# Right operands of 256 columns, high and low parts on two sides of the left ones

## The chip, the cores and the metric

The kernel runs on one core of one Trainium2 chip. The metric is the device time of one execution in microseconds (us). Matrix products run on TensorE (PE in the profile; its weight loads are listed as PEld), element-wise work on VectorE (DVE) and ScalarE (ACT), a few small steps on GpSimd (POOL), and transfers are issued from the queues of SyncE (SP) and GpSimd. A matmul has a left (stationary) operand of 128 columns, which a weight load brings into the array, and a right (moving) operand of up to 512 columns, which is streamed through it. Both are read from the on-chip memory of 128 partitions; the sum is written to one of eight accumulation banks.

## The reference

One layer of a decoder block on 512 tokens of width 1,024, in float32:

```python
h = rmsnorm(x, pre_mix_norm)
q_r, k_r, v_r, g_r, q_s, k_s, v_s, gate_r, gate_s = split(h @ w_in)
ret = silu(g_r) * groupnorm(retention(q_r, k_r, v_r))
swa = windowed_attention_with_sinks(q_s, k_s, v_s)
merged = sigmoid(gate_r) * (ret @ w_ret_out) + sigmoid(gate_s) * (swa @ w_swa_out)
x = x + rmsnorm(merged @ w_out, post_mix_norm)
h = rmsnorm(x, pre_mlp_norm)
x = x + rmsnorm(relu(h @ w_up) ** 2 @ w_down, post_mlp_norm)
```

The weights are read once; the page counts 114.96 MB read from the chip's main memory in all.

## The kernel before

**Products in three parts.** To keep float32 accuracy at a faster rate of the array, every large operand is held as two tiles of a rounded format: a high part, and a low part that is the difference to the original. `split` (lines 135 and 136) makes the two: ACT copies into the high part, DVE subtracts. `mm3` then issues three matmuls into one accumulation group: left high by right high (line 179), left high by right low (line 180), left low by right high (line 181). So of every three matmuls two stream the high right part and one the low right part. Each has a weight load of its own.

**Strassen-like products.** The gates (`w_gate`), the up projection (`w_up`) and the values and gate of the retention (`w_v`, `w_g`) save one product in eight by working on 2 x 2 blocks with sums of blocks. In `wino_pair` the weights are the left operand and the activations, in blocks of 256 tokens, the right one: seven products of 4 x 3 = 12 matmuls with 256 columns, 84 in a pair. For the gates the right operands are quadrants of `hT` (the normalized input, transposed) and the four sums of quadrants in `hsum`; for the up projection they are `h2c`, `h2d` and the sums in `h2s`. There are 8 pairs of gates and 13 pairs in the up projection; the first three pairs of the latter run in plain form (`first_ups`, tile `up`, 288 matmuls with 256 columns), with `h2b`, `h2c` and `h2d` as right operands, and begin before the second half of the tokens is ready.

**Where else these tiles are used.** `hT` is also the right operand, with 512 columns, of the query and key projections of the retention (`project_block`, tile `pblk`), 192 matmuls; the same function serves the attention's queries with `xg`. In `wide` the roles are turned round: `hT` and `hsum` are the left operands, and weights with 512 columns (`whi`, `wlo`) are streamed, 336 matmuls.

**Order.** TensorE works through one stage after the other: keys and queries (ptok, pblk), retention values and gate (wide) with the attention in between, retention (ret_st, ret_v), attention output (ys), then in turn a pair or two of gates (wino) and retention output projections (yr, 512 columns), the output projection (ps), first ups (up), 13 up pairs (wino), the down projection (p, p4c). A planner orders each engine's instructions from their dependencies and priorities; the operands of a pair are prepared on ACT and DVE while the pair before is multiplied.

**Places in memory.** Tiles lie in pools, one behind the other in each partition. `pad(pool, size)` (line 109) allocates a tile that nobody uses, only to shift what follows. All other large tiles have sizes that are multiples of 256 bytes per partition, so a tile's place modulo 256 bytes is set by the pads in front of it alone. In the kernel before, the weights (`whi`, `wlo`, `p24`, `p22`) begin at the same place modulo 256; both parts of `hT`, `hsum`, `h2b`, `h2c`, `h2d` and `h2s` begin 64 bytes in front of that place. In the last stage (`p`, `p4c`), in `yr`, `ys`, `ps`, `ret_st`, `ret_v` and for `xg`, left and right operands begin at the same place.

Of the kernel before, what the change touches and what calls it, by code (L numbers as in the profile page):

```python
# [11 lines left out]
F32R = mybir.dt.float32r  # L12
# [4 lines left out]
P = 128  # L17
D_MODEL = 1024
SEQ = 512
NT = SEQ // P  # L20
KD = D_MODEL // P
# [73 lines left out]
def block_kernel(ctx, tc, x, xT, pre_mix, w_in, w_v, w_g, w_gate, w_ret, w_swa, w_out, sinks, post_mix,  # L95
# [13 lines left out]
    def pad(pool, size, name="pad"):  # L109

        pool.tile([P, size // 4], F32, name=name, bufs=1)
# [7 lines left out]

    pad(const, 192)  # L120
    nc.scalar.mul(early, mhalf, 1.0)

    def rstd_of(sumsq, n, scale):

        ms = small.tile([P, 4], F32, name="ms")
        r = small.tile([P, 4], F32, name="rstd")
        nc.vector.tensor_scalar(ms[:, :n], sumsq, scale, EPS, op0=ALU.mult, op1=ALU.add)
        nc.gpsimd.tensor_tensor(r[:, :n], ms[:, :n], mhalf[:, :n], op=ALU.pow)
        return r
# [56 lines left out]
    def wino_pool(stack, side="left"):  # L186
        return stack.enter_context(tc.tile_pool(name="wx", bufs=1, side=side))
# [108 lines left out]
    hctx = ExitStack()  # L296
    hpool = hctx.enter_context(tc.tile_pool(name="hpool", bufs=1))
    pad(hpool, 192)
    hT = [hpool.tile([P, KD, SEQ], F32R, name=f"hT{i}") for i in range(2)]
    hsum = [hpool.tile([P, 4, 4, 256], F32R, name=f"hsum{i}") for i in range(2)]  # L300

# [698 lines left out]
    h2pool = uctx.enter_context(tc.tile_pool(name="h2pool", bufs=1))  # L1002
    h2spool = uctx.enter_context(tc.tile_pool(name="h2spool", bufs=1))
    pad(h2pool, 192)
    h2c = [h2pool.tile([P, 2, 4, 256], F32R, name=f"h2c{i}") for i in range(2)]
    h2d = [h2spool.tile([P, 4, 256], F32R, name=f"h2d{i}") for i in range(2)]
    h2s = [h2spool.tile([P, 4, 4, 256], F32R, name=f"h2s{i}") for i in range(2)]
    rspool = uctx.enter_context(tc.tile_pool(name="rspool", bufs=1))
    px = uctx.enter_context(tc.tile_pool(name="px", bufs=1))
    pad(px, 64)  # L1010
    wx = wino_pool(uctx)
    pctx = ExitStack()
    ppool = pctx.enter_context(tc.tile_pool(name="ppool", bufs=1))
    pad(ppool, 192)
    h2b = [ppool.tile([P, 4, 256], F32R, name=f"h2b{i}") for i in range(2)]
    quads = [
        [tuple(a[:, 0] for a in h2c), tuple(h2b)],
        [tuple(a[:, 1] for a in h2c), tuple(h2d)],
# [347 lines left out]
```

## Time and profile before

| | |
|---|---|
| median of 3 timed runs | 723.2 us (722.64 to 727.7) |
| span of the profiled execution | 719.9 us |
| TensorE busy | 708.3 us, 98%, 4,438 matmuls |
| weight loads busy | 628.8 us, 87% |
| DVE, ACT busy | 535.8 us (74%), 421.7 us (59%) |
| matmuls with 256 columns | 2,316 of the 4,438 are of the three-part form |

The page of a profile gives busy times of the engines, the chain of work that ended last, and groups of equal instructions. Groups of TensorE list the tile written, the tiles read, the count and the duration of one. Matmuls are pipelined: one starts before the one before it has ended, so the duration of one (276 ns, say) is longer than the distance from its start to the next one's start. The distance is read from the timeline.

### The profile page before, as it was taken

What the parts mean: (1) busy time and instruction counts of PE and PEld (TensorE: products, weight loads), DVE (VectorE), ACT (ScalarE), POOL (GpSimd) and SP (SyncE); (2) the same over time, 40 slices, a digit from 0 to 9 for tenths busy, and PEclk for the clock granted to TensorE, in tenths of its full rate; (3) what the DMA queues carried; (4) which work ended last, traced back from release to release, by engine and by line L of the source; (5) the groups of instructions that cost most, each with busy time, mean ns of one, the idle gap of its engine ahead of it and who ended that gap; (6) DMA issues with size and microseconds to landing.
All of it is one profiled execution on the core that took longest, in us unless ns stands there. A gap on an engine that the chain in (4) does not pass through costs nothing.

```text
span 719.9 us, 11248 instructions
## 1 busy us (share of the span) xinstructions
PE 708.3 (98%) x4438; PEld 628.8 (87%) x4438; DVE 535.8 (74%) x808; ACT 421.7 (59%) x712; POOL 60.3 (8%) x75
## 2 busy tenths in 40 slices
PE   8999999999999999999999999999999999999996
PEld 7877878888888989989888999999999888888885
DVE  5699986667885667566845876877776788977797
ACT  6667676345665526344643776666668666655571
POOL 0200000201100000000002100000000110010010
PEclk9999999999999999999999999999999999999999
DMA  9964424916444455461563618777753999698603
GB/s 318 330 179 84 108 72 129 282 46 132 101 142 120 107 162 147 125 197 59 198 271 117 159 47 234 201 202 193 204 153 118 305 278 238 151 208 194 118 0 117
DMA packets 43605, 117.79 MB, mean 164 GB/s; under 512 B 3488, under 2 KB 21024, under 8 KB 37408
## 3 DMA queue, kind: packets, MB, share of 16 engines
q1 hardware_dynamic: 36784, 80.76, 31.8%
q0 software_dynamic: 6480, 36.18, 27.3%
q8 instruction: 35, 0.57, 0.3%
q14 instruction: 18, 0.15, 0.1%
q10 hardware_dynamic: 288, 0.14, 0.1%
HBM read 114.96 MB, written 2.10 MB: 163 GB/s over the span
## 4 chain that ended last, share of the span: by engine, by line
PE 79%; DVE 8%; DMA 5%; ACT 4%; issue 2%; POOL 0%; POOLq 0%; DVEq 0%; SPq 0%; ACTq 0%
PE wino L179 9%; PE wino L180 9%; PE wino L181 9%; PE p L181 5%; PE p L180 5%; PE p L179 5%; DVE wlo L136 3%; PE wide L179 3%; PE wide L180 3%; PE wide L181 3%; DMA raw<-in_w_in 3%; PE ps L180 2%; PE ps L181 2%; PE yr L181 2%; PE yr L180 2%; PE yr L179 2%
## 5 line engine op out<-in xcount | busy, mean ns | idle before, releaser
L136 DVE TENSOR_TENSOR wlo<-raw,whi 128x1024 fp32r<-128x1024 f32 x81 | 98.6, 1223 | 42.4 <-ACT whi L135 42.2
L135 ACT CAST whi<-raw 128x1024 fp32r<-128x1024 f32 x81 | 84.8, 1052 | 40.4 <-DMA raw<-in_w_down 7.6
L181 PE MATMUL p<-whi,left 128*128 128x512 f32 x216 | 84.1, 390 | 0.2 <-DVE left L136 0.2
L180 PE MATMUL p<-wlo,left 128*128 128x512 f32 x216 | 84.2, 390 | 0.0
L179 PE MATMUL p<-whi,left 128*128 128x512 f32 x216 | 84.0, 390 | 0.1
L181 PEld LDWEIGHTS p<-whi,left 128*128 128x128 f32 x216 | 40.5, 188 | 9.3 <-DVE left L136 1.0
L180 PEld LDWEIGHTS p<-wlo,left 128*128 128x128 f32 x216 | 40.5, 188 | 8.9 <-DVE wlo L136 0.4
L179 PEld LDWEIGHTS p<-whi,left 128*128 128x128 f32 x216 | 40.5, 188 | 8.7 <-ACT left L135 0.5
L136 DVE TENSOR_TENSOR wlo<-tch,whi 128x1024 fp32r<-128x1024 f32 x32 | 38.6, 1220 | 6.9 <-ACT whi L135 6.9
L135 ACT CAST left<-uc 128x1024 fp32r<-128x1024 f32 x28 | 29.3, 1050 | 23.4 <-PE p L180 23.4
L135 ACT CAST p<-rs 128x1024 fp32r<-128x1024 f32 x21 | 22.1, 1051 | 35.5 <-DVE rs L230 35.4
L136 DVE TENSOR_TENSOR left<-uc,left 128x1024 fp32r<-128x1024 f32 x28 | 34.1, 1221 | 10.4 <-ACT left L135 10.4
L135 ACT CAST whi<-tch 128x1024 fp32r<-128x1024 f32 x32 | 33.2, 1050 | 11.3 <-PE p L181 6.8
L136 DVE TENSOR_TENSOR p<-rs,p 128x1024 fp32r<-128x1024 f32 x21 | 25.7, 1226 | 15.4 <-ACT p L135 15.4
L136 DVE TENSOR_TENSOR wlo<-rs,whi 128x1024 fp32r<-128x1024 f32 x21 | 25.7, 1224 | 12.1 <-ACT whi L135 9.4
L136 DVE TENSOR_TENSOR wlo<-acc,whi 128x1024 fp32r<-128x1024 f32 x20 | 24.1, 1217 | 6.5 <-ACT whi L135 6.5
L179 PE MATMUL wino<-h2s,p 128*128 128x256 f32 x104 | 28.7, 276 | 0.0
L180 PE MATMUL wino<-h2s,p 128*128 128x256 f32 x104 | 28.7, 276 | 0.0
L181 PE MATMUL wino<-h2s,p 128*128 128x256 f32 x104 | 28.7, 276 | 0.0
L179 PE MATMUL wino<-h2c,whi 128*128 128x256 f32 x104 | 28.7, 276 | 0.0
L180 PE MATMUL wino<-h2c,whi 128*128 128x256 f32 x104 | 28.7, 276 | 0.0
L181 PE MATMUL wino<-h2c,wlo 128*128 128x256 f32 x104 | 28.7, 276 | 0.0
(354 smaller groups left out, 2317.7 us busy)
## 6 DMA issues: line engine op xcount, KB each, us to landing
tch<-in_w_down POOLq DMA_DIRECT2D x12, 1024.0 KB, 9.5
raw<-in_w_down SPq DMA_DIRECT2D x7, 1024.0 KB, 7.6
rs<-in_w_up SPq DMA_DIRECT2D x13, 512.0 KB, 4.2
rs<-in_w_up POOLq DMA_DIRECT2D x13, 512.0 KB, 5.7
raw<-in_w_up SPq DMA_DIRECT2D x13, 512.0 KB, 5.1
raw<-in_w_in SPq DMA_DIRECT2D x8, 512.0 KB, 5.2
acc<-in_w_v POOLq DMA_DIRECT2D x4, 1024.0 KB, 7.9
rs<-in_w_gate SPq DMA_DIRECT2D x8, 512.0 KB, 3.9
```

Of the source, the lines that this page charges most:

```text
L135: last["hi"] = nc.scalar.copy(hi, src)
L136: last["split"] = nc.vector.tensor_tensor(lo, src, f(hi), op=ALU.subtract)
L179: nc.tensor.matmul(ps, ah, bh, start=first, stop=False, skip_group_check=more)
L180: nc.tensor.matmul(ps, ah, bl, start=False, stop=False, skip_group_check=more)
L181: nc.tensor.matmul(ps, al, bh, start=False, stop=last, skip_group_check=more)
```

## The change

A new helper allocates the two parts of a tile with a pad of 128 bytes between them, so that the second one lies 128 bytes further on modulo 256. Allocated in the order high, low, with the high part 64 bytes in front of the left operands, the low part comes to lie 64 bytes behind them. With `swap` the low part is allocated first; it is used where the pads so far have already moved the place by 128. The pad in front of `px` grows by 128, so that the weights that follow keep their place. The instructions, their order and the transfers are the same.

```diff
+    def two_sides(pool, shape, name, swap=False):
+
+        order = (1, 0) if swap else (0, 1)
+        t = {}
+        for i in order:
+            t[i] = pool.tile(shape, F32R, name=f"{name}{i}")
+            if i == order[0]:
+                pad(pool, 128, f"{name}pad")
+        return [t[0], t[1]]
...
-    hT = [hpool.tile([P, KD, SEQ], F32R, name=f"hT{i}") for i in range(2)]
-    hsum = [hpool.tile([P, 4, 4, 256], F32R, name=f"hsum{i}") for i in range(2)]
+    hT = two_sides(hpool, [P, KD, SEQ], "hT")
+    hsum = two_sides(hpool, [P, 4, 4, 256], "hsum", True)
...
-    h2c = [h2pool.tile([P, 2, 4, 256], F32R, name=f"h2c{i}") for i in range(2)]
-    h2d = [h2spool.tile([P, 4, 256], F32R, name=f"h2d{i}") for i in range(2)]
-    h2s = [h2spool.tile([P, 4, 4, 256], F32R, name=f"h2s{i}") for i in range(2)]
+    h2c = two_sides(h2pool, [P, 2, 4, 256], "h2c")
+    h2d = two_sides(h2spool, [P, 4, 256], "h2d", True)
+    h2s = two_sides(h2spool, [P, 4, 4, 256], "h2s")
...
-    pad(px, 64)
+    pad(px, 192)
...
-    h2b = [ppool.tile([P, 4, 256], F32R, name=f"h2b{i}") for i in range(2)]
+    h2b = two_sides(ppool, [P, 4, 256], "h2b")
```

## The prediction

> **What bounds the kernel now.** I read the page first: engines' busy shares, then the chain that ended last.
>
> ```profile
> span 719.9 us, 11248 instructions
> PE 708.3 (98%) x4438; PEld 628.8 (87%) x4438; DVE 535.8 (74%) x808; ACT 421.7 (59%) x712; POOL 60.3 (8%) x75
> ...
> PE 79%; DVE 8%; DMA 5%; ACT 4%; issue 2%; POOL 0%; POOLq 0%; DVEq 0%; SPq 0%; ACTq 0%
> ```
>
> TensorE is busy for 98% of the span and carries 79% of the chain. The profiled execution spans 719.9 us; the median of the timed runs, 723.2 us, is 3.3 us above that. I take this rest as fixed, so a difference of spans goes straight onto 723.2. The change moves operands and no instruction: no count, no transfer and no wait is added. It can act only through the rate at which matmuls follow each other, so next I read that rate, in the groups of TensorE alone. Columns: count, duration min/median/max in ns, first and last start.
>
> ```profile
> L179 PE MATMUL wino<-h2c,whi x104: 276/276/276, 435.0 to 551.6; 128*128 128x256 f32 x104
> L179 PE MATMUL wino<-hT,whi x64: 276/281/367, 232.1 to 336.3; 128*128 128x256 f32 x64
> L179 PE MATMUL p4c<-whi,left x16: 278/283/283, 707.1 to 712.5; 128*128 128x256 f32 x16
> ```
>
> The same instruction, 128x256, has three durations: 276, 281 and 283 ns. These are pipelined matmuls, so the price of one is the distance between starts, from the timeline (start in us, duration in us):
>
> ```profile
> 435.03 0.28 PE L179 MATMUL wino<-h2c,whi 128*128 128x256 f32 x1
> ...
> 557.43 0.39 PE L179 MATMUL p<-whi,left 128*128 128x512 f32 x1
> ...
> 262.63 0.28 PE L179 MATMUL wino<-hT,whi 128*128 128x256 f32 x1
> ...
> 282.42 0.39 PE L179 MATMUL yr<-retT,whi 128*128 128x512 f32 x1
> ...
> 707.12 0.28 PE L179 MATMUL p4c<-whi,left 128*128 128x256 f32 x1
> ...
> 712.74 0.28 PE L181 MATMUL p4c<-whi,left 128*128 128x256 f32 x1
> ```
>
> From 435.03 to 557.43 there are 1,080 steps (90 products of 12): 122.40/1080 = 113.3 ns. From 262.63 to 282.42 there are 168 (two pairs of 84): 19.79/168 = 117.8 ns. In the last block 47 steps take 5.62 us: 119.6 ns. So 276, 281 and 283 ns in a group stand for a spacing of about 113.3, 117.8 and 120 ns.
>
> What sets them apart? Not the clock: these windows have a granted clock of 1.00 (column PEclk) and a busy TensorE.
>
> ```profile
> 262.62:282.41 19.79, 19.79 (x169) 19.78 (x168) 13.32 (x18) 10.84 (x18) 1.74 (x2) 1.00 0.57 141
> 435.03:557.42 122.39, 122.39 (x1082) 122.39 (x1081) 90.96 (x117) 84.59 (x153) 9.64 (x11) 1.00 0.70 192
> ```
>
> (The counts include one or two matmuls that only stick into the window.) Nor is it the shape. What differs is the place of the operands: all tiles of the program are multiples of 256 bytes per partition, so the pads alone set the places. In p4c the right operand begins where the left one does, modulo 256; in the products on hT, hsum, h2b, h2c, h2d and h2s both parts of the right one begin 64 bytes in front of the left. So the place matters, worth 6.3 ns per matmul at best; but at one and the same place, −64, there are two rates, 113.3 and 117.8, and each holds through whole stretches. What was running just before decides. Behind 512-column matmuls (yr at 262, ps at 399) the gates and the first ups fall into 117.8; behind transposes they settle at 113.3:
>
> ```profile
> 232.04 0.19 PEld L179 LDWEIGHTS wino<-hT,whi 128*128 128x128 f32 x1
> 232.15 0.19 PEld L180 LDWEIGHTS wino<-hT,whi 128*128 128x128 f32 x1
> ...
> 399.92 0.28 PE L179 MATMUL up<-h2c,whi 128*128 128x256 f32 x1
> ...
> 408.40 0.28 PE L179 MATMUL up<-h2c,whi 128*128 128x256 f32 x1
> ...
> 410.88 0.28 PE L179 MATMUL up<-h2c,whi 128*128 128x256 f32 x1
> ```
>
> 399.92 to 408.40 is 72 steps at 117.8; from 410.88, behind the transposes of h2, to 435.03 it is 213 steps at 113.4. I read this as a lock of two streams: while a matmul streams its right operand, the weight load of the next reads its left one; where they meet in the memory one waits, and the waits shift the phase until a pattern repeats.
>
> **How much there is to gain.** The pair above at 232 also shows the floor: two weight loads that wait for no stream of a matmul are 0.11 us apart. In the fast lock a load follows its matmul's start at once and the matmul follows the load by 0.11 us:
>
> ```profile
> 439.79 0.28 PE L179 MATMUL wino<-h2d,p 128*128 128x256 f32 x1
> 439.79 0.19 PEld L180 LDWEIGHTS wino<-h2d,p 128*128 128x128 f32 x1
> 439.90 0.28 PE L180 MATMUL wino<-h2d,p 128*128 128x256 f32 x1
> ```
>
> So 113.3 is the loads' own chain with 3 ns beside it. No arrangement gets 256-column matmuls far under it.
>
> **The change part by part.** Right operands concerned: gates 8 pairs x 84 = 672, first ups 288, 13 up pairs x 84 = 1,092; 2,052 matmuls. In each group of three (high·high, high·low, low·high, lines 179 to 181) only the second streams a low right part, so 684 of them move from −64 to +64; the others stay, but the phase in which they find the loads changes. Now they cost 577 x 117.8 (six pairs of gates and 73 ups) + 1,475 x 113.3 = 68.0 + 167.1 = 235.1 us.
>
> (1) Lock. +64 does not occur with 256 columns in this trace; its nearest rows have 512.
>
> ```profile
> 192.17 0.40 PE L181 MATMUL wide<-whi,hsum 128*128 128x512 f32 x1
> ...
> 206.82 0.39 PE L179 MATMUL ys<-swaT,whi 128*128 128x512 f32 x1
> ...
> 42.92 0.39 PE L179 MATMUL pblk<-hT,whi 128*128 128x512 f32 x1
> ...
> 53.18 0.39 PE L181 MATMUL pblk<-hT,wlo 128*128 128x512 f32 x1
> ...
> 251.75 0.39 PE L179 MATMUL yr<-retT,whi 128*128 128x512 f32 x1
> ...
> 262.40 0.39 PE L181 MATMUL yr<-retT,wlo 128*128 128x512 f32 x1
> ```
>
> In wide (right 64 behind left) 64 steps take 14.65 us, 228.9 each; in pblk on hT (64 in front) 44 steps take 10.26 us, 233.2; in yr (same place) 47 steps take 10.65 us, 226.6. With 512 columns, then, −64 is the worst place by 6.6 ns, with 256 the best by 6.3, so these rows do not settle what +64 costs with 256: it can lie anywhere between the floor and the slow end (both are priced as rivals). I take the nearest row in shape and tiles: every product runs at the 113.3 that the same tiles reach now, since a right operand that changes sides breaks the slow pattern, in which the same meeting recurs. That saves 577 x 4.5 = 2.6 us.
>
> (2) hT is also the right operand of pblk: 192 matmuls, of which 64 stream the low part: 64 x (233.2 − 228.9) = 0.3 us saved; bounds 192 x 6.6 = 1.3 us saved and, with no row that excludes it, as much lost.
>
> (3) hT and hsum are the left operands of wide, 336 matmuls; the low left part of a third now lies 64 behind the right one: 112 x (233.2 − 228.9) = 0.5 us lost; bounds 336 x 2.3 = 0.8 saved, 336 x 4.3 = 1.4 lost.
>
> (4) The writers of the moved tiles (ACT and DVE at lines 135 and 136) issue the same instructions, and the pad before px restores the weights' places; bounded at zero by the cover in the window rows above: DVE is busy for 13.3 of 19.8 us and 91.0 of 122.4, and TensorE idles nowhere there. With gates 4% faster, that cover remains; were it gone, a step of theirs would show one for one.
>
> Sum: −2.6 − 0.3 + 0.5 = −2.4 us, 723.2 − 2.4 = 720.8 us.
>
> **The rivals.** *The lock is lost* (slower). If alternating sides keep the streams from settling, the right operand's stream is the bound and each matmul pays what its place costs. At the same place the two widths differ by 226.6 − 119.6 = 107.0 ns for 256 columns, so a bare stream takes an estimated 107.0 or 214.0 ns and the same place costs 12.6 in both; −64 costs 19.2 in pblk and +64 14.9 in wide. Two of the one and one of the other give 107.0 + 17.8 = 124.8 ns, 2,052 x 124.8 = 256.1, +21.0 us. The lower end is what every place pays at least, 119.6 ns: 245.4, +10.3 us; the middle is 122.2, +15.7: 739 us. That same place costs the same in both widths speaks for it; that −64 costs 19.2 with 512 and 6.3 with 256 speaks against it while the lock holds. It decides from 3.5 ns per matmul on, where 7.2 us are lost.
>
> *Only the low third pays*: the streams settle again behind each low product, which alone costs 107.0 + 14.9 = 121.9: 684 x 8.6 = +5.9, less the 2.6 of the lock: 727 us.
>
> *Fewer meetings than now*: the streams no longer meet at all. Transposes, whose 128 columns of plain float32 stream as long as 256 here, show the bound of a stream alone:
>
> ```profile
> 231.71 0.60 PE L790 MATMUL ret_t<-ident,retn 128*128 128x128 f32 x4
> ```
>
> (0.60 − 0.27)/3 = 0.109 us. At 109.5 all 2,052 cost 224.7, −10.4 us: 713 us; at 111.5, −6.3: 717. Against it stands the loads' chain of 110. The Trainium skill, page "TensorE: Matmul & The Clock Gate", section "Back-to-back issue gap", gives 262 cycles for 256 columns, an estimate of 109.2 ns; by it the sum would be −11 us, but the trace's 113.3 differs.
>
> *Nothing happens*: places explain none of it, and the rates follow from what ran before: 723.2 us. The same page, section "Step-by-step: what each phase is for", says just this: TensorE reads stationary and moving operand over two independent ports, and loading the next weights takes no bandwidth from the running matmul. By that rule the pads are worth nothing; the 119.6 of p4c beside the 113.3 of wino speaks against it.
>
> **How the numbers follow.** Forecast 0.37; only the low third pays 0.08; nothing 0.15; lock lost 0.31; fewer meetings 0.09. A measurement of this kernel can tell about 1%, 7.2 us, from no change: under 716.0 is faster, over 730.4 slower. Faster: most of the fewer meetings, 0.08. Slower: the lost lock, with a little of the low third, 0.32. Within: 0.60. The range runs from 716, past the bounds of (1) to (3) at their best (2.6 + 1.3 + 0.8 saved), up to 742, past the middle of the lost lock; out are the fewer meetings at their end (0.07) and the upper part of the lost lock (0.11). The likeliest cases alone lie within 717 to 728.
>
> **What would show it.**
>
> ```profile
> L179 PE MATMUL up<-h2c,whi x48: 276/281/281, 399.9 to 418.4; 128*128 128x256 f32 x48
> L179 PE MATMUL pblk<-hT,whi x64: 392/394/496, 42.0 to 160.1; 128*128 128x512 f32 x64
> L179 PE MATMUL wide<-whi,hsum x64: 388/392/505, 60.9 to 200.6; 128*128 128x512 f32 x64
> ```
>
> Step (1): group medians of wino on hT and of up at 276 instead of 281 ns, and 276 still for h2c and h2s. Medians of 283 or more, in line 180 alone or in all three, are the low third or the lost lock; under 276, fewer meetings. Steps (2) and (3): the medians of pblk and wide, 394 and 392 now, moving by under 5 ns. I would be wrong at once if the 13 up pairs took other than 122 to 123 us.

## The result, and the profile after

The changed kernel takes 732.77 us (median of 6 runs, 731.34 to 737.24). The kernel before took 727.3 us in the six runs beside them (722.64 to 727.7). The ratio is 1.0102, with a 95% interval of 1.0064 to 1.0139: slower by one per cent. The forecast, 720.8 us, is missed on the wrong side; the time lies in the range.

The page of the changed kernel (span, engines' busy time, chain of work that ended last):

```profile
span 730.4 us, 11246 instructions
PE 717.5 (98%) x4438; PEld 638.1 (87%) x4438; DVE 536.0 (73%) x808; ACT 421.8 (58%) x712; POOL 64.3 (9%) x75
...
PE 36%; DVE 4%; DMA 2%; issue 1%; ACT 1%; POOL 0%; POOLq 0%; DVEq 0%; ACTq 0%
```

VectorE and ScalarE do the same work in nearly the same time; TensorE has 9.2 us more of it (717.5 against 708.3) with the same 4,438 matmuls. The chain's shares add up to 44%: in this trace it could be followed back only to the middle of the execution, so I don't compare chains. I cut both executions at four matmuls that both have: the first of the gates, the first of `ps`, the first of the 13 up pairs, the first of `p4c`. From the timeline (start in us, duration in us), first the two of the kernel before that the prediction did not show, then the four of the changed one:

```profile
232.07 0.37 PE L179 MATMUL wino<-hT,whi 128*128 128x256 f32 x1
354.63 0.39 PE L179 MATMUL ps<-wo,mhi 128*128 128x512 f32 x1
```

```profile
233.04 0.37 PE L189 MATMUL wino<-hT,whi 128*128 128x256 f32 x1
...
356.15 0.39 PE L189 MATMUL ps<-wo,mhi 128*128 128x512 f32 x1
...
439.53 0.28 PE L189 MATMUL wino<-h2c,whi 128*128 128x256 f32 x1
...
568.03 0.28 PE L191 MATMUL wino<-h2s,p 128*128 128x256 f32 x1
...
717.64 0.28 PE L189 MATMUL p4c<-whi,left 128*128 128x256 f32 x1
```

| stretch | before, us | after, us | difference |
|---|---|---|---|
| start to first gate | 232.07 | 233.04 | +0.97 |
| gates and yr, to first `ps` | 122.56 | 123.11 | +0.55 |
| `ps` and first ups, to first up pair | 80.40 | 83.38 | +2.98 |
| up pairs and down projection, to `p4c` | 272.09 | 278.11 | +6.02 |
| `p4c` to the end | 12.8 | 12.8 | 0 |

The first row belongs mostly to this one execution: in the other profile of the changed kernel (below) the first gate starts at 232.21. Two things make up the rest. The first is the rate. From 439.53 to 568.03 the last matmul of the last up pair is 1,091 steps away: 128.50/1091 = 117.8 ns, where the kernel before ran at 113.3. From each start to the next it is 116.3, 119.6 and 117.5 ns on the three lines: the low product is the dearest step. The groups by tile (count, duration min/median/max in ns, first and last start) show it on each line:

```profile
L189 PE MATMUL wino<-h2c,whi x104: 278/280/281, 439.5 to 560.7; 128*128 128x256 f32 x104
L190 PE MATMUL wino<-h2c,whi x104: 282/282/283, 439.6 to 560.8; 128*128 128x256 f32 x104
L191 PE MATMUL wino<-h2c,wlo x104: 279/280/281, 439.8 to 561.0; 128*128 128x256 f32 x104
```

No median is 276 any more, nor is any 283: this is neither the forecast nor the lost lock as it was priced, but one mean rate for every group of three. The window of these pairs has the same granted clock as before, 1.00, and about the same cover on DVE (92.13 of 128.50 us).

```profile
439.53:568.03 128.50, 128.50 (x1094) 128.50 (x1092) 92.13 (x119) 85.16 (x153) 10.49 (x12) 1.00 0.66 182
```

The second is waits that the kernel before does not have. TensorE's waits in the changed kernel (us in total, times, longest):

```profile
PE p L189 <- ACT left L145: 1.1, 1, 1.1
PE up L189 <- DVE zg L994: 0.7, 1, 0.7
PE up L189 <- ACT h2c L145: 0.7, 1, 0.7
...
PE up L190 <- DVE h2c L146: 0.2, 1, 0.2
```

The first ups now wait for the writing of `h2c`, which itself begins later. The groups of the ACT line that writes it, before and after:

```profile
L135 ACT CAST h2c<-tin x4: 586/598/630, 393.6 to 395.5; 128x512 fp32r<-128x512 f32 x4
```

```profile
L145 ACT CAST h2c<-tin x4: 585/590/610, 401.6 to 404.5; 128x512 fp32r<-128x512 f32 x4
its engine sat idle before it (us, times) until:
  PE ps L191: 0.7, 1
```

It ran while `ps` was still being multiplied; now it waits for the last matmul of `ps`, eight us later. The cause is in the pads. The tiles of the `ps` stage and those of the up stage are laid into the same memory, one stack after the other, from the same byte on. The merged operand that `ps` reads begins 256 + 2 x 16,384 = 33,024 bytes behind that byte. The two tiles `h2c` end, in the kernel before, 16,384 + 192 + 2 x 8,192 = 32,960 bytes behind it: 64 bytes short. The new pad of 128 bytes between them takes the second one 64 bytes into a tile that `ps` reads to its end. In the same way three pads, 384 bytes, now lie in front of the end of `h2s`; it shares 320 bytes with the first of the `left` tiles, from which it was 64 bytes away, so the writing of that one waits for the last up pair. The planner put the instructions into another order around both: the last 12 matmuls of the up pairs, for one, stood behind the first of `p` and now stand in front of them. So the section on the change is wrong in saying that the order is the same.

### The profile page after: what moved, and what is told of

The parts are those of the page before. It is cut to its first block, busy times and chain, and to the rows that moved or that the text cites. A ratio compares the mean times of both kernels' runs of the same rounds, so it can differ in the third digit from the quotient of the medians.

```text
span 730.4 us, 11246 instructions
## 1 busy us (share of the span) xinstructions
PE 717.5 (98%) x4438; PEld 638.1 (87%) x4438; DVE 536.0 (73%) x808; ACT 421.8 (58%) x712; POOL 64.3 (9%) x75
## 5 line engine op out<-in xcount | busy, mean ns | idle before, releaser
L190 PE MATMUL wino<-h2s,p 128*128 128x256 f32 x104 | 29.4, 282 | 0.0
L190 PE MATMUL wino<-h2s,whi 128*128 128x256 f32 x104 | 29.4, 282 | 0.0
L191 PE MATMUL wino<-h2s,p 128*128 128x256 f32 x104 | 29.1, 280 | 0.0
L191 PE MATMUL wino<-h2s,wlo 128*128 128x256 f32 x104 | 29.1, 280 | 0.0
```

Of the source, the lines that this page charges most:

```text
L190: nc.tensor.matmul(ps, ah, bl, start=False, stop=False, skip_group_check=more)
L191: nc.tensor.matmul(ps, al, bh, start=False, stop=last, skip_group_check=more)
```

## The experiments

**The kernel before, once more.** No edit; the question is whether its rate is one.

> The kernel before, unchanged, looked at once more. Theory A (two locks): with both right parts 64 in front, the 13 up pairs run as a whole at 113.3 or as a whole at 117.8 ns per matmul, and this alone moves the execution by 1,092 x 4.45 = 4.9 us, so times of about 723 and about 727.5 both belong to this kernel. Theory B (the place alone sets the rate): the up pairs stand at 113.3 in every execution, and times of 727 have another cause, seen elsewhere in the trace.

Measured: 721.93 us (721.3 to 728.67, 10 runs), ratio 0.9976 (0.9937 to 1.0014) to the same kernel's other runs. The times lie in two groups: six of the ten at 721.3 to 721.93, four at 727.18 to 728.67. The profile fell on the execution of 728.51 us, and in it the up pairs run at the other rate: first up pair, and 1,080 steps later the first matmul of `p`:

```profile
437.16 0.28 PE L179 MATMUL wino<-h2c,whi 128*128 128x256 f32 x1
...
564.36 0.39 PE L179 MATMUL p<-whi,left 128*128 128x512 f32 x1
```

127.20/1080 = 117.8 ns, against 122.40/1080 = 113.3 in the first profile: 4.8 us. The same program has two rates on the same tiles, and which one it takes in the up pairs changes from execution to execution. That is what its times of 722 and 727.5 us are, as far as the two profiled executions show (719.9 and 726.7 us of span); a few of its other runs (724.2, 726.5, 731.6) belong to neither. The two executions part behind the transposes of `h2`: the 213 steps from there to the first up pair, at 113.4 ns in the prediction's lines, take 117.8 here, behind the same instructions. The place alone does not set the rate.

**Two sides for the up stage only.**

```diff
-    hT = two_sides(hpool, [P, KD, SEQ], "hT")
-    hsum = two_sides(hpool, [P, 4, 4, 256], "hsum", True)
+    hT = [hpool.tile([P, KD, SEQ], F32R, name=f"hT{i}") for i in range(2)]
+    hsum = [hpool.tile([P, 4, 4, 256], F32R, name=f"hsum{i}") for i in range(2)]
```

> Two sides for h2b, h2c, h2d and h2s alone; hT and hsum with both parts in front as before. Theory A: up and its 13 pairs at 117.8 with the three lines at 116.3, 119.6 and 117.5; the gates on hT and hsum at 113.3 or 117.8 as they fall. Against the kernel before +4.9 us and up to +1 in the first ups when that one has its fast lock, about nothing when it has its slow one. Theory B: the same rates in the up stage, gates at the rates of before; +6 us against every execution of before.

Measured: 731.15 us (730.54 to 732.87, 8 runs), ratio 1.0087 (1.0051 to 1.0124). The up stage alone carries nearly all of the loss, and it has both marks: 117.8 ns in the up pairs (116.2, 119.6 and 117.5 on the three lines, as both theories had it) and the waits. Neither theory had the waits: against the better group of the kernel before the loss is 9 us, not 5 or 6. This is the wait behind the up pairs:

```profile
568.42 0.50 PE L189 MATMUL p<-whi,left 128*128 128x512 f32 x1 [1.13 <-ACT left L145]
```

**Two sides for the gates only.**

```diff
-    h2c = two_sides(h2pool, [P, 2, 4, 256], "h2c")
+    h2c = [h2pool.tile([P, 2, 4, 256], F32R, name=f"h2c{i}") for i in range(2)]
...
-    pad(px, 192)
+    pad(px, 64)
```

`h2d`, `h2s` and `h2b` go back in the same way.

> Two sides for hT and hsum alone; the up stage as before. Both theories: gates at 117.8 in all eight pairs (before: two at 113.3), pblk 1.5 us shorter, wide 0.6 us longer. Theory A: the up stage on its own falls into 113.3 or 117.8; total within 1 us of the kernel before in the same lock. Theory B: up stage at 113.3.

Measured: 723.34 us (721.68 to 736.76, 10 runs), ratio 0.9996 (0.9957 to 1.0036). All eight gate pairs run at 117.8, also the first two, which the kernel before runs at 113.4; 154 steps by 4.4 ns are 0.7 us, and little of it is left at the end. The up pairs keep the kernel before's two rates; in the profiled execution they had the better one:

```profile
437.39 0.28 PE L189 MATMUL wino<-h2c,whi 128*128 128x256 f32 x1
...
559.79 0.39 PE L189 MATMUL p<-whi,left 128*128 128x512 f32 x1
```

122.40/1080 = 113.3 ns. Theory B, which expected this in every execution, fails on the three of ten at 727.76 to 728.18 us, if these are the worse rate as in the kernel before (no profile fell on one); the longest, 736.76 us, stands alone. The forecast for pblk, 1.5 us shorter, is missed: 0.3 us on the 144 matmuls from 100 to 180 us.

**Both parts behind.** All right operands 64 bytes behind the left ones, one side only.

```diff
-    pad(h2pool, 192)
+    pad(h2pool, 320)
...
-    pad(px, 64)
+    pad(px, 192)
```

The pads of `hpool` and `ppool` grow likewise, and pads behind them restore the places of the weights.

> Both parts of hT, hsum, h2b, h2c, h2d and h2s 64 bytes behind the left operands: the price of that place by itself. Theory A (a lock needs all three steps alike; both sides alike give one again): a single rate in all three lines, anywhere from 113.3 to 120. Theory B (a low part behind costs 119.6, its price in the changed kernel): 119.6 in all three lines, up pairs 1,092 x 119.6 = 130.6 us.

Measured: 731.04 us (one run). It has 117.8 ns everywhere: in the up pairs 279, 280 and 279 ns on the three lines. That is the one rate of theory A; theory B's 119.6 in all three lines is wrong. And it has the waits of the changed kernel, 0.7 us for `h2c` and 1.1 us for `left`, without any alternation of sides. So the waits come with the shift of the tiles, whatever the sides. These 128 bytes more in front of `h2c` also end 64 bytes inside what `ps` reads.

**The waits by themselves, put in and taken out.** The kernel before without two pads, that in front of the tiles of `ps` (`wpool`) and that in front of the `left` tiles (`junks`); the changed kernel with the two larger. Neither moves an operand modulo 256. As far as the traces show, the first has the changed kernel's order of instructions on every engine, and the second the order of the kernel before.

```diff
-    pad(wpool, 256)
...
-    pad(junks, 256)
```

> The kernel before with every operand at its own place modulo 256, but with two pads taken out (256 bytes in front of the tiles of the ps stage, 256 bytes in front of the ring of the left tiles): the second tile h2c then shares 192 bytes with a high tile of the merged operand that the last ps matmuls read, as it shares 64 bytes in the changed kernel, and the first left tile shares 192 bytes with the low tile of the sums that the last up pair reads, as it shares 320 bytes in the changed kernel. Theory W (shared memory is the second cause): the profile shows the two waits of the changed kernel (PE waits about 0.7 us for the writing of h2c at the start of the up stage, stalls of about 950 and 600 ns there, one of about 1,400 ns after the last up pair), the matmul rates stay those of the kernel before (113.3 or 117.8 ns), and the time is 2.0 to 3.0 us over the kernel before: ratio 1.003 to 1.004. Rival N (the stalls come with the other places of the h2 tiles, or are won back behind): no such waits, ratio 1.000.

```diff
-    pad(wpool, 256)
+    pad(wpool, 512)
...
-    pad(junks, 256)
+    pad(junks, 768)
```

> The changed kernel with every operand at its place on two sides, but with the pad in front of the tiles of the ps stage 256 bytes larger and the one in front of the left tiles 512 bytes larger, so that neither pair of tiles shares memory any more. Theory W: the waits are gone (no PE wait for h2c, no stall of 1,400 ns after the last up pair), the single rate of 117.8 ns stays on every matmul of 256 columns, and the time is 2.0 to 3.0 us under that of the changed kernel: 728 to 730 us. What is left over the kernel before is then the rate alone: 4.45 ns for those matmuls that the kernel before runs at 113.3 (about 1,090 of the up pairs in its faster executions, 214 of the first ups, 154 of the gates: 6.5 us), less 1 us on the 512-column stages: ratio 1.003 to 1.007. Rival N: the stalls stay and the time is that of the changed kernel.

The changed kernel ran beside them, unedited:

> The changed kernel itself, on the same chip as the runs beside it. Every theory expects 731 to 733 us and one rate, 117.8 ns, for every matmul of 256 columns on the h tiles; its executions lie in one group (within 2 us), since there is one rate only, where the kernel before has two groups, 722 and 727.5 us.

Measured, in this order: 727.19 us (724.52 to 733.22, 10 runs; ratio 1.0028, 0.9993 to 1.0063), 728.27 us (727.42 to 729.69, 10 runs; 1.0035, 1.0008 to 1.0062), 732.19 us (730.73 to 734.22, 8 runs; 1.0086, 1.0055 to 1.0118). Of the last two, no run of one reaches the range of the other: without the shared bytes the changed kernel is 3.9 us faster. That is 0.9 us over the upper end of what I expected. The changed kernel's own runs spread over 3.5 us where 2 were expected. The kernel without shared bytes has the order of the kernel before and no such wait, and still its up pairs run at 117.8 ns, with the same durations as in the changed kernel:

```profile
L190 PE MATMUL wino<-h2c,whi x104: 282/282/283, 436.4 to 557.6; 128*128 128x256 f32 x104
```

So the rate comes from the places and not from the order. In the profile of the kernel before with shared memory the waits stand at their places, while the up pairs run at 113.3 (timeline, then the group by tile):

```profile
409.04 0.50 PE L179 MATMUL up<-h2c,whi 128*128 128x256 f32 x2 [0.68 <-ACT h2c L135]
...
410.21 0.38 PE L179 MATMUL up<-h2c,whi 128*128 128x256 f32 x1 [0.67 <-DVE zg L983]
```

```profile
L179 PE MATMUL wino<-h2c,whi x104: 276/276/277, 445.2 to 561.8; 128*128 128x256 f32 x104
```

So waits and rate are two independent costs. The interval of this run includes 1, so its times alone don't show the cost of the waits: the two rates of the kernel before spread its times by more than the waits are worth. Its lowest time, 724.52 us, is 3.4 us above the lowest of the kernel before beside it, 721.14. In its profile the stretch from `ps` to the first up pair takes 82.27 us against 80.40, and that from there to `p4c` 273.54 against 272.09. (This execution, 733.22 us, is long for another reason: TensorE waits once 6.4 us for `wlo` ahead of the gates.) The four matmuls of the changed kernel without shared bytes, and the three of the changed kernel beside it that differ:

```profile
232.17 0.37 PE L189 MATMUL wino<-hT,whi 128*128 128x256 f32 x1
...
355.01 0.39 PE L189 MATMUL ps<-wo,mhi 128*128 128x512 f32 x1
...
436.33 0.28 PE L189 MATMUL wino<-h2c,whi 128*128 128x256 f32 x1
...
713.37 0.28 PE L189 MATMUL p4c<-whi,left 128*128 128x256 f32 x1
```

```profile
355.64 0.39 PE L189 MATMUL ps<-wo,mhi 128*128 128x512 f32 x1
...
439.01 0.28 PE L189 MATMUL wino<-h2c,whi 128*128 128x256 f32 x1
...
717.14 0.28 PE L189 MATMUL p4c<-whi,left 128*128 128x256 f32 x1
```

From `ps` to the first up pair it is 81.32 against 83.37 us, from there to `p4c` 277.04 against 278.13: the stall at the first ups costs 2.05 us, the one on `left` 1.09 us. The first holds the three waits of the list above; the one put down to `zg` comes and goes with the other two, and why it is there is not shown. This 3.1 us is what one pair of executions shows in place; the rest of the 3.9 is not placed.

**Turns ahead of each pair.** A transposition (called a turn below) into the first accumulator, ahead of each of the 21 pairs of the kernel before; so each pair is a new entry, a start behind something other than its own kind.

```diff
+        nc.tensor.transpose(chain[:, :P], ident, ident)
         product(chain, "11", "11")
```

> The kernel before with one transposition of 128 columns into the first accumulator right ahead of each gate pair and each up pair (21 of them); nothing else moved. Theory T (which of the two rates a stretch takes is settled when the product is entered, and entered behind a transposition it is mostly the fast one): the gate pairs 3 to 8, which the kernel before ran at 117.8 ns behind the 512-column matmuls of yr, run at 113.3 ns (504 matmuls by 4.45: 2.2 us less), the up pairs run at 113.3 ns in nearly every execution, and each turn costs about 0.13 us (2.7 us): 722.4 us in one group, with the group at 727.5 us gone or rare. Rival P (the rate is set by something outside, for the whole execution): gate pairs 3 to 8 stay at 117.8 ns and the times lie in two groups at 724.6 and 730 us.

Measured: 729.74 us (728.18 to 731.96, 10 runs), ratio 1.0041 (1.001 to 1.0072). Neither theory: the rate is indeed settled anew at each entry, but mostly the worse one comes out. Three turns in a row:

```profile
455.90 0.27 PE L263 MATMUL wino<-ident 128*128 128x128 f32 x1
...
465.90 0.27 PE L263 MATMUL wino<-ident 128*128 128x128 f32 x1
...
475.55 0.27 PE L263 MATMUL wino<-ident 128*128 128x128 f32 x1
```

The first pair takes 10.00 us with its turn, the next 9.65. With 84 matmuls in each, 0.35 us are 4.2 ns per matmul, the two rates. By the distances between starts 6 of the 21 pairs settle at 113.3, 15 at 117.8; among the 13 up pairs it is the fourth, fifth, ninth and tenth. Theory P falls too: pairs of one execution differ.

**A 512-column matmul ahead of each pair.**

```diff
+        w0 = a["11"][0]
+        nc.tensor.matmul(p25.rearrange("p a c -> p (a c)"), w0[:, 0], w0.rearrange("p k c -> p (k c)"), start=True, stop=True, skip_group_check=True)
         product(chain, "11", "11")
```

> The kernel before with one matmul of 512 columns at the same place as its left operand (a weight block against its own tile, written into a bank that the pair overwrites) right ahead of each gate pair and each up pair, where the experiment with the transpositions had its turns. Theory T (the rate is settled when a stretch is entered, and behind a 512-column matmul it is always the slow one, as behind yr and ps): all 21 pairs run at 117.8 ns, none at 113.3, and with 21 matmuls by 0.23 us the time is 731 to 733 us. Rival D (the entry is a draw, whatever stands ahead, with the odds of the turns, 6 of 21 fast): about 6 of the 21 pairs at 113.3 ns.

Measured: 735.09 us (one run), 2 us over what theory T expected. By the distances between starts 20 of the 21 pairs run at 117.8; the exception is the first, whose 512-column matmul came after a gap, at 113.6. All 104 matmuls of this group show the one rate:

```profile
L179 PE MATMUL wino<-h2c,whi x104: 281/281/281, 440.0 to 563.9; 128*128 128x256 f32 x104
```

So theory T holds as to what decides, the entry; rival D's odds of 6 in 21 do not. The gates' worse rate in the kernel before is that of their entry behind `yr`. But a 512-column matmul right ahead does not always give the worse rate: in the profile of the kernel before, once more, the last 12 matmuls of the up pairs, entered behind a `p`, begin at 117 ns and go over to 113 after five steps. And a transposition did not secure the better one.

**Other distances.** Three kernels with both parts at one distance: 128 bytes, 32 bytes in front, 96 bytes in front. The edit is that of the kernel with both parts behind, with other sizes; for 96 bytes in front it is

```diff
-    pad(h2pool, 192)
+    pad(h2pool, 160)
...
-    pad(px, 64)
+    pad(px, 96)
```

> The kernel before with all right operands of 256 columns 128 bytes from the left ones modulo 256, the farthest there is, high and low alike; no two tiles newly share memory, and the order of instructions on every engine is that of the kernel before. Theory S (the spacing is a whole number of steps of 6.67 ns, 17 or 18 for one matmul, or a mix of them, and the place decides which mixes exist): mean spacings of 113.3, 115.6, 117.8 or 120.0 ns and nothing between; if distance is what helps, 113.3 ns alone and about 720 us. Rival U (what is measured at 64 bytes in front is a property of that distance only): 117.8 or 120.0 ns everywhere and 728 us or more.

> The kernel before with all right operands of 256 columns 32 bytes in front of the left ones modulo 256, half the distance of the kernel before; nothing else moved, same order of instructions. Theory S: mean spacings of 113.3, 115.6, 117.8 or 120.0 ns and nothing between; nearer to the same place, so 117.8 to 120.0 ns, 728 to 732 us. Rival U: as at 64 bytes in front, both 113.3 and 117.8 ns stretches.

> The kernel before with all right operands of 256 columns 96 bytes in front of the left ones modulo 256; nothing else moved, same order of instructions. Theory S: mean spacings of 113.3, 115.6, 117.8 or 120.0 ns and nothing between; farther away than in the kernel before, so 113.3 in at least as many stretches, 720 to 723 us. Rival U: 117.8 ns everywhere, 728 us.

Measured, one run each: 730.24, 730.01 and 731.18 us. First up pair, and the first matmul of `p` 1,080 steps later, in this order:

```profile
438.06 0.28 PE L179 MATMUL wino<-h2c,whi 128*128 128x256 f32 x1
...
566.23 0.39 PE L179 MATMUL p<-whi,left 128*128 128x512 f32 x1
```

```profile
438.27 0.28 PE L179 MATMUL wino<-h2c,whi 128*128 128x256 f32 x1
...
566.07 0.39 PE L179 MATMUL p<-whi,left 128*128 128x512 f32 x1
```

```profile
438.92 0.28 PE L179 MATMUL wino<-h2c,whi 128*128 128x256 f32 x1
...
567.08 0.40 PE L179 MATMUL p<-whi,left 128*128 128x512 f32 x1
```

128.17, 127.80 and 128.16 us over 1,080 steps: 118.7, 118.3 and 118.7 ns. No gate pair and no up stretch of these three executions settles at 113.3. Theory S expected only 113.3, 115.6, 117.8 or 120.0: wrong, there are values between. Rival U is wrong for 32 bytes in front, where it expected the two rates of 64, and half right for the others: slow, but in the up pairs at a rate that is neither 117.8 nor 120.0. Distance is not what helps: 96 bytes in front has not shown the better rate of 64. With one execution at each distance, a second rate that was not met is not excluded.

**Twenty-one entries for each arrangement of sides.** The same 21 turns, in the changed kernel without shared bytes, with both parts behind, and with the sides swapped, for which the changed kernel's pads in front become those of the kernel with both parts behind:

```diff
+        nc.tensor.transpose(chain[:, :P], ident, ident)
         product(chain, "11", "11")
```

```diff
-    pad(h2pool, 192)
+    pad(h2pool, 320)
...
-    pad(px, 192)
+    pad(px, 64)
```

> The changed kernel without the shared memory, with the 21 transpositions ahead of the gate pairs and up pairs: 21 fresh entries at different moments. Theory A (with parts on both sides there is one rate only): all 21 pairs at 117.8 ns, 353.3 ns for three matmuls, whatever the entry; 731 us (the 728 to 729 us of the kernel without turns and 2.7 us for them). Rival E (the fast rate exists there too and was missed, its odds are only lower): some of the 21 pairs at 113.3 ns, as 6 of 21 were on one side.

> Both parts of the right operands 64 bytes behind the left ones modulo 256, without the shared memory, with the same 21 transpositions. Theory H (the fast rate belongs to 64 bytes in front; a part that lies behind can't be in it): all 21 pairs at 117.8 ns. Rival A2 (uniform places have both rates on either side, and it is the alternation alone that takes the fast one away): about 6 of 21 pairs at 113.3 ns, as in front.

> The two sides the other way round, high parts 64 bytes behind and low parts 64 bytes in front, without the shared memory, with the same 21 transpositions. Theory A: one rate, 117.8 ns in all 21 pairs, as for the changed kernel; the three lines of a product change their shares, their sum of 353.3 ns stays. Rival H2 (the rate goes by how many of the three matmuls lie behind, two of three here, one of three in the changed kernel): another sum than 353.3 ns.

Measured, one run each: 731.67, 732.24 and 732.15 us. One group by tile, the products of high by high part on `h2c`, first of the kernel before with turns, then of these three in their order:

```profile
L179 PE MATMUL wino<-h2c,whi x104: 276/281/367, 435.9 to 557.1; 128*128 128x256 f32 x104
```

```profile
L189 PE MATMUL wino<-h2c,whi x104: 278/281/367, 437.9 to 560.6; 128*128 128x256 f32 x104
```

```profile
L179 PE MATMUL wino<-h2c,whi x104: 279/279/366, 437.2 to 559.9; 128*128 128x256 f32 x104
```

```profile
L189 PE MATMUL wino<-h2c,whi x104: 278/281/365, 438.1 to 560.7; 128*128 128x256 f32 x104
```

The 276 ns that stands for the better rate is in the first row alone. By the distances between starts none of the 63 pairs settles at 113.3; the means are 117.8, but for one pair of the swapped kernel at 117.1. Of the places tried, only both parts 64 bytes in front has therefore shown the rate of 113.3 ns. It is not the alternation that takes it away: a uniform place behind takes it away too. So theories A and H hold, and rivals E, A2 and H2 fall. Which part lies behind changes the three lines (117.1, 119.0 and 117.4 ns in the up pairs with the low part behind; 118.4, 116.6 and 118.4 with the high part behind), but not their sum.

## Why the prediction was wrong

**The sum.** Two steps failed, and the base was taken from one of two kinds of execution.

**Step (1), the lock: wrong in its reason.** It said that a right operand that changes sides breaks the slow pattern. It takes away the fast one. All 2,052 matmuls run at about 117.8 ns: 241.7 us against the 235.1 of the prediction's sum, 6.6 us lost where 2.6 were to be gained. The two-sided kernel showed no second rate, neither in 21 entries nor in ten runs without the shared bytes, which lie within 2.3 us. The price of place −64 was read rightly as two rates, and behind 512-column matmuls as the worse one; "behind transposes they settle at 113.3" was true of the two entries in that trace and is no rule: the same entry behind the transposes of `h2` gave 117.8 in the next profile, and with turns 6 of 21 entries gave 113.3. I had no row for +64 with 256 columns, took the value of the tiles where they lay, and that choice was the error; the row nearest in kind, the other rate of the same tiles, was in the trace.

**"No count, no transfer and no wait is added", and step (4): wrong.** The matmuls and the transfers stayed; the order did not. And a pad moves where a tile ends, and with memory used in turn its end decides for whom its writer waits. Two stalls appeared, 2.05 and 1.09 us where they stand, 3.9 us between the medians. The cover that step (4) named, DVE's idle time in windows of the gates and of the up pairs, was of the wrong places: at `h2c` the writer runs between the end of `ps` and the first ups, where TensorE waits for it.

**Steps (2) and (3).** Right in sign and, for pblk, in size. In the stretch from 100 to 180 us, where all pblk matmuls are on `hT`, TensorE is busy with 144 of them for (first value after the window's length), before and after:

```profile
100.00:180.00 80.00, 34.94 (x144) 26.57 (x144) 0.00 (x0) 3.48 (x6) 1.00 0.51 135
```

```profile
100.00:180.00 80.00, 34.66 (x144) 26.60 (x144) 0.00 (x0) 3.49 (x6) 1.00 0.50 133
```

0.28 us less on 144, which is 0.37 on all 192, where 0.3 was forecast. The mechanism is right too: from the start of the low product to the next it is 228.9 ns on `hT` instead of 233.6, the rate that the prediction took over from wide. For wide, the 64 steps that took 14.65 us now take 14.93, from the first of these rows of the changed kernel to the second:

```profile
192.86 0.39 PE L191 MATMUL wide<-whi,hsum 128*128 128x512 f32 x1
...
207.79 0.39 PE L189 MATMUL ys<-swaT,whi 128*128 128x512 f32 x1
```

That is 4.4 ns for each: here all three lines pay, and not only the third with the low left part. The distances of all 336 add up to 0.6 us more than before (78.31 to 78.88), so elsewhere it is less. That the sum comes near the forecast 0.5 is luck.

**The base.** 723.2 us was the median of three runs of a kernel with times near 722 and near 727.5. Six of its runs have 727.3 as median, so the same change costs some 10 us against one group and 5 against the other. The two profiles of the kernel before put 4.8 us of that into the up pairs. Against an execution with the worse rate there, the changed kernel loses almost only its waits: without them it takes 728.3 us.

**The rivals.** *The lock is lost* gave the right sign with the wrong price: one step of three pays 119.6, the one at the low product, but the mean of the three is 117.8, below the rival's lower end. Its lower end, +10.3 us, comes near the measured time only because of the waits, which it did not have; so it is by luck that the measured time lies where this rival put the range. *Only the low third pays*: the low product is the dearest step, but the other two cost 116.3 and 117.5, not 113.3, and the sum of three lines is that of the worse rate of one side, so there is no third rate. *Fewer meetings* falls, since no stretch runs under 113.3. *Nothing happens* falls by the ten runs without shared bytes, which form one group, and by the 21 entries without the better rate; that the up pairs moved from 113.3 to 117.8 would not show it alone, since the kernel before makes that move too. The Trainium skill, page "TensorE: Matmul & The Clock Gate", section "Step-by-step: what each phase is for", lets the two operands be read over independent ports; by it all the distances tried would cost the same, and the trace disagrees with 113.3, 117.8, 118.3 and 118.7 ns for the same instruction. That two reads meet in the memory remains an argument, though: no row here shows a read being held up, and what fixes the rate at an entry stays open.

**The announced signs** did their work: "wrong at once if the 13 up pairs took other than 122 to 123 us" was met by 128.5 us over 1,091 steps. But the kernel before meets this sign as well in its longer executions (127.2 us over 1,080 steps), so alone it could not tell the change from the entry; the ten runs without shared bytes and the 21 entries can.

## What to carry to other kernels

A pad has two effects: the place of what follows, and where it ends in memory that another stage has just used. Before one is added, compare the new ends with the tiles that are still read there; 64 bytes too many cost 2 us here, and a pad in front of the older stack gave them back. And time a kernel often enough to see whether its executions form one group or several before a gain of one per cent is sought in it: here the rate of a stretch is settled at its entry, and 4.8 us hang on that.

## What the runs showed of the hardware that was not expected

Matmuls of 256 columns with their left operand at one place follow each other at distances that depend on where the right one begins, modulo 256 bytes: 119.6 ns at the same place (prediction), 118.3 at 32 in front, 113.3 or 117.8 at 64 in front, 118.7 at 96 in front, 117.8 at 64 behind (at 32, 96 and 128 from one execution each). At 128 there are two again, 118.7 in the up pairs and, in gate pairs behind `yr`, 120.0:

```profile
263.29 0.28 PE L179 MATMUL wino<-hT,whi 128*128 128x256 f32 x1
...
283.45 0.39 PE L179 MATMUL yr<-retT,whi 128*128 128x512 f32 x1
```

20.16/168 = 120.0 ns. Such a rate, once entered, held for more than a thousand matmuls, and in the executions profiled it changed within a stretch only in the first dozen or so steps or at a stall. With the 21 turns it returned in a pattern, two of the better rate in every five up pairs, so it need not be chance. With one side in front, 113.3 is 17 and 120.0 is 18 times 6.67 ns, and 117.8 is the mean of 17, 18 and 18; the 512-column rates of the prediction, 226.6 and 233.2, are 34 and 35 times as much. That is a regularity of the numbers; what stands behind it no run here shows. Nor do the runs separate, with 256 columns, the place of the right operand from its distance to the left one, since only the right one moved. With 512 columns the left one's place counts by itself: in wide the right operand stayed where it was, and 64 steps went from 14.65 to 14.93 us.
